# A hybrid decoder layer: weights and x loaded in half blocks in the order of use, adaLN summed by VectorE and TensorE, and the list schedule's durations corrected

## The chip, the cores and the metric

The kernel runs on one core of one Trainium2 chip. The metric is the device time of one execution in microseconds. TensorE, VectorE, ScalarE, GpSimd and SyncE appear in the rows as PE, DVE, ACT, POOL and SP; SP issues most of the DMAs, ScalarE's queue a few small ones.

## What is computed

One layer on x of 4096 tokens by 1024 features, float32. The condition c gives, through a 1024 x 3072 matrix (`ada_w`), a shift, a scale and a gate:

```python
shift, scale, gate = jnp.split(c_act @ ada_w + ada_b, 3, axis=-1)
h = _rmsnorm(x, g_pre) * (1.0 + scale[:, None]) + shift[:, None]
proj = h @ w_in
...
y = jnp.concatenate([attn, rwkv, gla], axis=-1) @ w_out
return x + gate[:, None] * _rmsnorm(y, g_post)
```

Between the two lies a mixer of three groups of heads that all read h: sliding-window attention (window 128), RWKV-7 (a delta rule, in chunks of 64 tokens) and gated linear attention (GLA).

## The kernel before

The tokens are worked in 16 chunks of 256. A first half of the kernel makes h for each chunk, the RWKV and GLA projections and both recurrences, and leaves h (`hscr`) and the mixed heads (`mscr`) in DRAM. A second half reads h again and does attention, the gates, the output projection and the final norm. Every float32 weight is split into two float16 halves, a high and a low (`kh`, `kl` and so on), and so is h (`hT`): a projection is three matmuls per block of 128 features. A split of a weight (`load_w`) squares and sums it on ScalarE, sums over the partitions with a matmul by ones (`wssp`), makes a power of two from that on VectorE (`pow2`, a chain of operations of one column: `wtot`, `p2e`, `p2f`, `wsc`), writes the high half with ScalarE and the low half with VectorE.

Before the first chunk stands a start. The weights' blocks of 256 columns (1 MB each) come through four big buffers (`stg`: two with the tag AT, two with the tag hT). Eight blocks of `ada_w` are summed by VectorE, one step per block of 128 rows (`acc`), and a matmul by ones finishes each (`adp`). From them come `sh` and `gs`, and a common power of two, `hscale`. Then follow the splits of `gv` and `gk1` (GLA values and gate), `L` (the two low-rank inputs of RWKV, made from `wlt`), `k`, `r`, `v` and `gqk`. `wlt` lies in the only buffer of x (`xt`). The gate's four blocks of `ada_w` (`stage_g`) are multiplied and folded by GpSimd (`aw`, `acc`), summed with a matmul (`gp`), copied by VectorE (`gr`) and stored (`gscr`).

A chunk's stages: `stage_a` loads x, takes its norm (`ssx`, `msx`, `rsx`: a short chain on VectorE), scales x in place, transposes it on TensorE (`tp`), applies `gs` and `sh` on ScalarE (`hf`) and splits it into `hT`. `stage_p` does the projections: `pv` (gv and gk1), `lp` (L), `zz` three times (k, r, v), `gqk`; `stage_d` the decays, the other stages the recurrences. `cs` are pieces of the second half's weights, split on the way (`stage_c`).

The order of the work is made twice. `emit` runs the stages as generators and picks, by a rough model of the engines (`Model`, `Lane`), which goes on next; that fixes the order in which instructions are written. Each is noted in `Order` (`note`) with a duration, what it needs and its buffers. `pin` then schedules all that were noted with these durations, engine by engine, always the first written among those that are ready, and fixes each engine's order by dependencies without a semaphore. It is called once after the first half and once at the end. So a number in `note` moves instructions, and does no work itself. All instructions are recorded through one helper, line 299 before and 319 after, and so all rows have that line.

Of the kernel before, what the change touches and what calls it, by code (L numbers as in the profile page):

```python
# [16 lines left out]
ALU = mybir.AluOpType  # L17
# [16 lines left out]
LIFT = {}  # L34
LANES = ((0.06, 1.04e-3, VL), (0.02, 1.0e-3, AL), (0.1, 2.3e-3, 0.0), (0.0, 1e-3 / 2.4, PL), (0.05, 0.0, 2.0))
# [3 lines left out]
HOP_FROM = {"PE": 0.037, "DVE": 0.034, "Activation": 0.034, "Pool": 0.06, "SP": 0.03}  # L39
# [15 lines left out]
class Step:  # L55


    __slots__ = ("ins", "eng", "occ", "lat", "table", "array", "bytes", "needs", "turn", "start", "end", "left", "then")


class Order:
# [3 lines left out]
    def __init__(self, tc):  # L65
        self.tc, self.held, self.masks = tc, {}, {}
        self.steps = []
        self.wrote, self.read, self.users, self.slots, self.known = {}, {}, {}, {}, set()
# [26 lines left out]
    def note(self, eng, name, outs, ins, func, r):  # L95

        st = Step()
        st.ins, st.eng, st.table, st.array, st.bytes, st.then = r.ins, str(eng.engine).split(".")[-1], None, None, 0, []
        e, o = st.eng, outs[0]
# [3 lines left out]
        if e == "PE":  # L103
# [7 lines left out]
            took = max(took, 0.056 if not f32 else 0.109 if mode[1] == 4 else 0.0)  # L111
# [4 lines left out]
        elif e == "SP":  # L116
# [3 lines left out]
            st.lat = next((t for k, t in ((8, 1.9), (64, 2.0), (128, 2.2), (256, 2.6), (512, 3.5)) if kb <= k), 4.8)  # L120
# [32 lines left out]
        out_r, in_r = [self.region(a) for a in outs], [self.region(a) for a in ins]  # L153
        tiles = {a.tensor.name: a.tensor for a in [*outs, *ins]}
# [53 lines left out]
    def pin(self):  # L208
# [10 lines left out]
        cells, mode, table, pipe = [0.0] * 16, None, None, 0.0  # L219
        last = {}  # L220
        for _ in steps:
            e = min((e for e in ENGINES if ready[e]), key=lambda e: max(free[e], min(ready[e].values())))
            now = max(free[e], min(ready[e].values())) + 1e-9
            k = min(k for k, t in ready[e].items() if t <= now)
# [10 lines left out]
            else:  # L235
                if st.table is not None and st.table != table:
                    t, table = max(t, free[e] + 1.28), st.table
                free[e], st.end = t + st.occ, t + st.lat
                if st.bytes > 100e3:
                    pipe = max(pipe, t + 1.7) + st.bytes / 310e3  # L240
                    st.end = max(st.end, pipe)
# [22 lines left out]
class Model:  # L264


    def __init__(self, tc):
        self.tc, self.lift, self.order = tc, 0, Order(tc)
        self.wrote, self.read, self.banks = {}, {}, {}
        self.now = 0.0  # L270
# [15 lines left out]
class Lane:  # L286
# [6 lines left out]
    def __getattr__(self, name):  # L293
        f = getattr(self.eng, name)

        def call(*args, **kw):
# [6 lines left out]
            accum = kw.get("accum_out")  # L303
            self.model.order.note(self.eng, name, aps[:1] + ([] if accum is None else [accum]),
# [31 lines left out]
            end = t + took + self.late  # L336
            for o in outs:
                m.wrote[o] = (end, self)
# [18 lines left out]
def hybrid_kernel(ctx, tc, x, vecs, rows, adaw, w1, wl, w2, wo, w2aug, a2, gk2, cst, ctr, ctg, abias, out):  # L357
# [149 lines left out]
    def emit():  # L507

        while live:
# [13 lines left out]
            model.lift = LIFT.get(best[2], 0)  # L523
# [18 lines left out]

    def ada_block(eng, acc, aw, cc):

        SP.dma_start(aw, adaw[cc])
        if eng is V:
            V.tensor_scalar(acc, aw[:, 0, :], scol[:, 0:1], None, op0=ALU.mult)
            for k in range(1, KD):
                V.scalar_tensor_tensor(acc, aw[:, k, :], scol[:, k : k + 1], acc, op0=ALU.mult, op1=ALU.add)
        else:  # L550
            eng.tensor_tensor(aw, aw, scol.rearrange("p (k o) -> p k o", o=1).to_broadcast([P, KD, 256]), op=ALU.mult)
            eng.tensor_tensor(aw[:, 0:4, :], aw[:, 0:4, :], aw[:, 4:8, :], op=ALU.add)
            eng.tensor_tensor(aw[:, 0:2, :], aw[:, 0:2, :], aw[:, 2:4, :], op=ALU.add)
            eng.tensor_tensor(acc, aw[:, 0, :], aw[:, 1, :], op=ALU.add)
# [52 lines left out]
    with ExitStack() as p1:  # L607
# [26 lines left out]

        stc = itertools.count()

        def stage_tile(width=256):
            if next(stc) % 4 < 2:
                t = t_A([P, 2048], "stg")
            else:  # L640
                t = t_hT("stg").rearrange("p a k n -> p (a k n)").bitcast(F32)
            return t.rearrange("p (k c) -> p k c", k=KD)
# [24 lines left out]


        adp = pst("at", "adp")
        for cc in (4, 5, 6, 7, 0, 1, 2, 3):  # L670
            acc = cs1([P, 256], "acc")
            ada_block(V, acc, stage_tile(), cc)
            for jj in range(2):
                j = 2 * cc + jj
                PE.matmul(adp[:, j : j + 1], acc[:, jj * P : (jj + 1) * P], ones[:, 0:1], start=True, stop=True)
        V.tensor_add(sh, adp[:, 0:8], vcol("bsh"))
# [13 lines left out]


        Wt = {}
        wlt = t_x("wlt")[:, 0, :].rearrange("p (k c) -> p k c", k=KD)
        SP.dma_start(wlt, wl)

        def gen_l(s32):
            for k in range(KD):
                V.tensor_scalar(s32[:, k, 128:192], wlt[:, k, 0:64], vcol("muw", k), None, op0=ALU.mult)
                V.tensor_scalar(s32[:, k, 192:256], wlt[:, k, 64:128], vcol("mua", k), None, op0=ALU.mult)
            V.tensor_sub(s32[:, :, 0:128], wlt, s32[:, :, 128:256])  # L700

        gvh = wk1[0].tile([P, KD, 272], F16, name="gvh")
        gvl = wk1[0].tile([P, KD, 272], F16, name="gvl")
        for n, name in ((0, "gv"), (5, "gk1"), (None, "L"), (2, "k"), (3, "r"), (4, "v"), (1, "gqk")):
            inv = cp.tile([P, 1], F32, name="iv" + name)
            if name == "gk1":
                Wt[name] = (gvh, gvl, inv)
                load_w(gvh[:, :, 256:272], gvl[:, :, 256:272], inv, wt([P, KD, 16], "gk1s", 1, tag="gl"), src=w1src(n))
            elif name == "gv":
                Wt[name] = (gvh, gvl, inv)  # L710
                load_w(gvh[:, :, 0:256], gvl[:, :, 0:256], inv, stage_tile(), src=w1src(n))
            else:
                Wt[name] = (wslot(name + "h"), wslot(name + "l"), inv)
                if name == "L":
                    load_w(*Wt[name], stage_tile(), gen=gen_l)
                else:
                    load_w(*Wt[name], stage_tile(), src=w1src(n))
            V.tensor_scalar(inv, inv, hinv, None, op0=ALU.mult)
        gq_s = cp.tile([P, 1], F32, name="gq_s")
        V.tensor_single_scalar(gq_s, Wt["gqk"][2], 32.0 ** -0.5, op=ALU.mult)  # L720
        mu_s = pp.tile([P, 6], F32, name="mu_s")
        mu_c = pp.tile([P, 6], F32, name="mu_c")
        V.tensor_scalar(mu_c, vcol("mu"), -1.0, 1.0, op0=ALU.mult, op1=ALU.add)
        for n, nm in enumerate("rkv"):
            js = slice(2 * n, 2 * n + 2)
            V.tensor_scalar(mu_s[:, js], vcol("mu")[:, js], Wt[nm][2], None, op0=ALU.mult)
            V.tensor_scalar(mu_c[:, js], mu_c[:, js], Wt[nm][2], None, op0=ALU.mult)
# [92 lines left out]
        def stage_g(_):  # L820

            for n in range(4):
                acc = cs1([P, 256], "acc")
                aw = t_A([P, KD, 256], "aw")
                ada_block(G, acc, aw, 8 + n)
                gp2 = mq("gp2")
                PE.matmul(gp2[:, :256], ones, acc, start=True, stop=True)
# [979 lines left out]
```

## Time and profile before

| | us |
|---|---|
| median of 3 runs | 2227.8 (2226.26 to 2230.65) |
| profiled execution, own time | 2226.16 |
| its span, first to last instruction | 2224.4 |
| TensorE busy | 2063.7 (93%) |
| VectorE busy | 1513.7 (68%) |
| ScalarE busy | 1111.6 (50%) |
| GpSimd busy | 191.6 (9%) |
| mean DMA rate | 85 GB/s |

A timeline row gives the start and the duration in microseconds, the engine, the line, the operation, what is written and read, the shapes and a count; in brackets stands how long the engine idled before it and what ended that. A count of float32 matmuls in the trace is twice that of the program, since each is recorded as two passes. A window's row gives for each engine its busy time and instructions, then the granted clock of TensorE (1.00 is full), the share of the DMA engines and their rate.

### The profile page before, as it was taken

Reading aid. Unit: us, or ns where it says so; the run is one execution under the profiler, and the core shown is the slowest. Engines: PE = TensorE matmul, PEld = TensorE weight load, DVE = VectorE, ACT = ScalarE, POOL = GpSimd, SP = SyncE. Lnnn points to the kernel's source line nnn. Section 1 sums busy time; section 2 is a strip of 40 time slices with the busy share of each in tenths; the row PEclk is TensorE's granted clock in tenths of the full one; section 3 lists DMA queues with packets and bytes.
Section 4 is the critical chain, followed back from the end, with each engine's and each line's share of the span. In section 5 each row is a group of like instructions: output and inputs, shape, how many; then the busy total and the mean of one; then the engine's idle time right before and its main releaser. Section 6 shows DMA issues by size and latency. Waiting matters only on the chain. (4 is left out here: it accounts for less than half of the span.)

```text
span 2224.4 us, 61651 instructions
## 1 busy us (share of the span) xinstructions
PE 2063.7 (93%) x25417; PEld 1755.6 (79%) x25417; DVE 1513.7 (68%) x4970; ACT 1111.6 (50%) x2627; POOL 191.6 (9%) x364
## 2 busy tenths in 40 slices
PE   1599999999999999999997999999999999999996
PEld 1478877777777777787776888888888888888885
DVE  7767787777778777666665676666666666666764
ACT  3566666676766765555423434343434434343441
POOL 0241100111111111111000000000000000000000
PEclk9899999999999999999998999999999999999998
DMA  7332233323233322102324121222221121212111
GB/s 292 118 100 94 80 97 100 97 88 111 77 103 102 97 90 71 54 16 76 124 76 137 63 89 51 70 70 76 71 78 62 56 68 67 78 69 80 61 42 38
DMA packets 149092, 188.46 MB, mean 85 GB/s; under 512 B 49458, under 2 KB 120648, under 8 KB 142408
## 3 DMA queue, kind: packets, MB, share of 16 engines
q1 hardware_dynamic: 146776, 182.23, 24.9%
q8 instruction: 201, 3.29, 0.6%
q10 hardware_dynamic: 2032, 2.26, 0.3%
q14 instruction: 83, 0.68, 0.1%
HBM read 126.75 MB, written 57.68 MB: 83 GB/s over the span
## 5 line engine op out<-in xcount | busy, mean ns | idle before, releaser
L299 PEld LDWEIGHTS <-mT 128*128 128x128 f16 x3072 | 301.3, 98 | 40.1 <-ACT mT L299 2.6
L299 ACT ACTIVATE pr<-pr,nm,lsc 128x256 f32<-128x256 f32 (+1 forms) x256 | 149.3, 585 | 88.7 <-DVE nm L299 86.7
L299 ACT ACTIVATE ag<-gp,gh 128x512 f32<-128x512 f32 x64 | 43.6, 682 | 185.5 <-PE gp L299 185.4
L299 PEld LDWEIGHTS <-hT 128*128 128x128 f16 x1536 | 119.5, 100 | 18.9 <-DVE hT L299 1.0
L299 DVE CUSTOM_DVE_ANT_0 pr<-sc,ab,sinks 128x256 f32<-128x256 f32 (+1 forms) x256 | 107.8, 477 | 37.6 <-PE sc L299 35.9
L299 DVE SCALAR_TENSOR_TENSOR ag<-ag,gp 128x512 f32<-128x512 f32 x64 | 43.5, 679 | 110.7 <-ACT ag L299 110.6
L299 PE MATMUL pv<-gvh,hT 128*128 128x272 f16 x512 | 100.4, 287 | 0.7 <-DVE hT L299 0.4
L299 PE MATMUL lp<-hT,Lh 128*128 128x256 f16 x512 | 96.1, 279 | 2.4 <-ACT vg L299 2.4
L299 PE MATMUL op<-o0h,mT 128*128 128x256 f16 x512 | 93.4, 276 | 3.6 <-ACT mT L299 2.5
L299 PE MATMUL zz<-hT,kh 128*128 128x256 f16 x512 | 92.3, 276 | 0.0
L299 PE MATMUL gp<-hT,q3h 128*128 128x256 f16 x512 | 88.0, 278 | 3.6 <-PEq L1669 3.6
L299 PE MATMUL op<-o3h,mT 128*128 128x256 f16 x512 | 91.4, 273 | 0.0
L299 ACT ACTIVATE jy<-yv 128x1024 f16<-128x1024 f32 x32 | 33.8, 1057 | 114.0 <-DVE yv L299 114.0
L299 PE MATMUL gqk<-hT,gqkh 128*128 128x256 f16 x512 | 88.1, 273 | 1.9 <-DVE zb L299 1.9
L299 PE MATMUL qp<-hT,q1h 128*128 128x256 f16 x512 | 85.5, 274 | 4.2 <-DVE kT L299 4.2
L299 PE MATMUL op<-o2h,mT 128*128 128x256 f16 x512 | 89.3, 273 | 0.0
L299 PE MATMUL op<-o1h,mT 128*128 128x256 f16 x512 | 89.1, 273 | 0.0
L299 POOL COPY kT<-kT 128x512 f16<-128x512 f16 x15 | 10.1, 676 | 909.6 <-DVE kT L299 853.1
L299 PE MATMUL zz<-hT,rh 128*128 128x256 f16 x512 | 86.7, 273 | 0.0
L299 PE MATMUL zz<-hT,vh 128*128 128x256 f16 x512 | 86.4, 273 | 0.0
L299 ACT ACT_TABLE_LOAD x65 | 83.4, 1283 | 5.4 <-DMA sinks<-in_rows 4.2
L299 PE MATMUL gp<-hT,q4h 128*128 128x256 f16 x512 | 85.7, 273 | 0.0
(385 smaller groups left out, 6318.8 us busy)
## 6 DMA issues: line engine op xcount, KB each, us to landing
xt<-in_x SPq DMA_DIRECT2D x16, 1024.0 KB, 5.0
hscr<-hT SPq DMA_DIRECT2D x16, 1024.0 KB, 7.0
hT<-hscr SPq DMA_DIRECT2D x16, 1024.0 KB, 4.8
xo<-in_x SPq DMA_DIRECT2D x16, 1024.0 KB, 5.5
out<-yv SPq DMA_DIRECT2D x32, 512.0 KB, 3.0
cs<-in_w SPq DMA_DIRECT2D x112, 128.0 KB, 2.2
stg<-in_adaw SPq DMA_DIRECT2D x8, 1024.0 KB, 7.6
cs<-in_wo SPq DMA_DIRECT2D x64, 128.0 KB, 2.2
```

What stands on the lines that cost most here:

```text
L299: r = f(*args, **kw)
```

## The change

Three things are changed together.

The start. Weights and adaLN blocks come in halves of 0.5 MB through eight buffers (`half_tile`: the buffers that chunk 0 uses later for RA, UV, KB and AT), in the order in which they are used: gv, gk1, `wlt`, x of chunk 0, then adaLN, then k, r, v, gqk. VectorE sums six blocks of adaLN; blocks 5 and 1 go to TensorE as matmuls of one column against `scol` (`adp<-scol,stg`). The splits of gv, gk1 and L (`early`) and the norm of x are written between the adaLN steps. The splits of k, r, v and gqk become a stream of their own (`stage_l`), and the gate's sums (`stage_g`) use eight halves in place of four blocks. Chunk 0's transposes use four PSUM banks.

```diff
+        RING = ("RA", "UV", "KB", "RA", "AT", "AT", "AT", "AT")
...
+        gvp = w_pieces(0)
+        gks = wt([P, KD, 16], "gk1s", 1, tag="gl")
+        SP.dma_start(gks, w1src(5))
+        wlt = half_tile().rearrange("p (k c) -> p k c", k=KD)
+        SP.dma_start(wlt, wl)
+        load_x(0)
...
-        for cc in (4, 5, 6, 7, 0, 1, 2, 3):
+        first = early()
+        for n, cc in enumerate((4, 5, 0, 6, 7, 1, 2, 3)):
+            if cc in PE_BLOCKS:
+                for jj in range(2):
+                    aw = half_tile().rearrange("p (k c) -> p k c", k=KD)
+                    SP.dma_start(aw, adaw[cc, :, :, jj * P : (jj + 1) * P])
+                    for k in range(KD):
+                        PE.matmul(adp[:, 2 * cc + jj : 2 * cc + jj + 1], aw[:, k, :], scol[:, k : k + 1], start=(k == 0),
+                                  stop=(k == KD - 1))
+                    next(first, None)
+                continue
             acc = cs1([P, 256], "acc")
-            ada_block(V, acc, stage_tile(), cc)
+            for h in range(2):
+                aw = half_tile().rearrange("p (k c) -> p k c", k=4)
+                SP.dma_start(aw, adaw[cc, :, 4 * h : 4 * h + 4, :])
...
-            for n in range(4):
-                acc = cs1([P, 256], "acc")
-                aw = t_A([P, KD, 256], "aw")
-                ada_block(G, acc, aw, 8 + n)
+            for n in range(8):
+                aw = half_tile("AT").rearrange("p (k c) -> p k c", k=KD)
+                SP.dma_start(aw, adaw[8 + n // 2, :, :, (n % 2) * P : (n % 2 + 1) * P])
+                acc = cs1([P, P], "acc")
...
+        streams((9, "l", stage_l, None))
```

The list schedule. A ready instruction is no longer taken by the place at which it was written alone, but by that place and a lag: those of `stage_l` count as 150 places later, those of `stage_g` as 500 (`LAG`). Where TensorE would have to change its tiling, it takes a ready instruction of the present tiling first (for up to 0.6 in the schedule's time, if that is the full array). Some durations are corrected, of which two lines show the kind, and VectorE and ScalarE get a small pause where the half of the partitions changes.

```diff
-HOP_FROM = {"PE": 0.037, "DVE": 0.034, "Activation": 0.034, "Pool": 0.06, "SP": 0.03}
+HOP_FROM = {"PE": 0.037, "DVE": 0.034, "Activation": 0.034, "Pool": 0.06, "SP": 0.6}
...
-            k = min(k for k, t in ready[e].items() if t <= now)
+            at = sorted((k for k, t in ready[e].items() if t <= now), key=lambda k: (steps[k].rank, k))
+            k = at[0]
+            if e == "PE" and mode is not None and steps[k].array[0] != mode:
```

The model of `emit`. Large loads share one DMA rate there in the first half (`m.pipe`).

How the instructions move is shown at three places. First SP's queue at the start, before (`in_adaw` is `ada_w`, `in_w` the weights):

```order
L299 DMA stg<-in_adaw 128x2048 x4
L299 DMA wlt<-in_wl 128x1024
L299 DMA gk1s<-in_w 128x128
L299 DMA cs<-in_w 128x256 x2
L299 DMA stg<-in_adaw 128x2048 x3
L299 DMA cs<-in_w 128x256 x2
L299 DMA stg<-in_adaw 128x2048
L299 DMA stg<-in_w 128x2048
L299 DMA cs<-in_w 128x256 x2
L299 DMA stg<-in_w 128x2048 x2
L299 DMA xt<-in_x 128x2x1024
```

and now, the first two being gv:

```order
L319 DMA stgRA<-in_w 128x1024
L319 DMA stgUV<-in_w 128x1024
L319 DMA gk1s<-in_w 128x128
L319 DMA stgKB<-in_wl 128x1024
L319 DMA xt<-in_x 128x2x1024
L319 DMA stgRA<-in_adaw 128x1024
L319 DMA stg<-in_adaw 128x1024
L319 DMA stg<-in_adaw 128x8x128 x2
```

gv, `wlt` and x have moved ahead of all of adaLN.

Second VectorE's queue where x of chunk 0 is scaled, before (it stands behind adaLN, between the splits of L and k):

```order
L299 SCALAR_TENSOR_TENSOR rsx<-nwt,rsx 128x2
L299 TENSOR_TENSOR nwt<-rsx 128x2
L299 SCALAR_TENSOR_TENSOR nwt<-nwt,msx 128x2
L299 SCALAR_TENSOR_TENSOR rsx<-nwt,rsx 128x2
L299 TENSOR_SCALAR xt<-xt,rsx 128x1024 x2
L299 SCALAR_TENSOR_TENSOR kl<-stg,wsc,kh 128x2048
```

and now:

```order
L319 TENSOR_SCALAR acc<-stgUV,scol 128x256
L319 TENSOR_SCALAR xt<-xt,rsx 128x1024
L319 SCALAR_TENSOR_TENSOR acc<-stgUV,scol,acc 128x256
L319 TENSOR_SCALAR xt<-xt,rsx 128x1024
L319 SCALAR_TENSOR_TENSOR acc<-stgUV,scol,acc 128x256 x2
L319 SCALAR_TENSOR_TENSOR acc<-stgKB,scol,acc 128x256 x3
```

The scaling has moved in among the adaLN steps, with half of them still to come.

Third TensorE's queue in chunk 0's projections, before, in the projection of k (`cgp` belongs to GLA's decay; the gate's sums `gp<-acc` stand one by one further back, in the projections of k, r and gqk):

```order
L299 MATMUL zz<-hT,kh 128x256
L299 MATMUL tp<-ident,xt 128x128 x4
L299 MATMUL cgp<-CTG,gl 128x129 x2
L299 LDWEIGHTS kh
L299 MATMUL zz<-hT,kh 128x256
```

and now, between the last matmul of k's projection and the first of r's (`tp` is of chunk 1):

```order
L319 MATMUL zz<-hT,kl 128x256
L319 MATMUL gp_476<-acc,ones 128x128
L319 MATMUL wssp<-wss_655,ones 128x2
L319 MATMUL gp_487<-acc,ones 128x128
L319 MATMUL tp<-ident,xt 128x128 x4
L319 MATMUL zp<-ident,vg 17x128 x2
L319 MATMUL gp<-gk2s,zlT 128x128 x2
L319 MATMUL gp_499<-acc,ones 128x128
L319 MATMUL tp<-ident,xt 128x128 x4
L319 MATMUL gp_510<-acc,ones 128x128
L319 LDWEIGHTS rh
L319 MATMUL zz<-hT,rh 128x256
```

Four of the gate's eight sums now stand together ahead of the whole projection of r, and chunk 1's transposes and decay stand among them.

More of the change, by code (lines that the diff above doesn't have):

```diff
@@ L702, in hybrid_kernel @@
[L702 to L718, printed above, removed]
```

190 lines of the change are left out of this document (136 added, 54 removed).

## The prediction

> **What bounds the kernel now.** I read the stages first (busy time by window), then what TensorE waits for, then the start instruction by instruction.
>
> ```profile
> span 2224.4 us, 61651 instructions
> core 0: us, PE busy (x) PEld busy (x) DVE busy (x) ACT busy (x) POOL busy (x), PEclk, DMA share, GB/s
> 20.00:25.00 5.00, 1.01 (x4) 0.93 (x4) 4.75 (x11) 0.91 (x4) 0.00 (x0) 1.00 1.04 423
> 0.00:62.40 62.40, 13.55 (x53) 11.87 (x54) 49.26 (x172) 23.39 (x43) 3.31 (x18) 1.00 0.75 280
> 79.00:97.00 18.00, 2.64 (x23) 2.13 (x23) 17.58 (x15) 2.05 (x6) 16.57 (x9) 0.76 0.43 157
> 97.00:136.20 39.20, 36.97 (x273) 30.70 (x274) 22.55 (x42) 21.59 (x43) 16.52 (x14) 0.89 0.21 81
> 136.20:1085.00 948.80, 908.32 (x12144) 741.14 (x12141) 696.47 (x2529) 598.83 (x1386) 136.69 (x292) 0.99 0.28 85
> 1254.00:2190.00 936.00, 924.15 (x10710) 825.08 (x10707) 604.84 (x1808) 385.39 (x971) 8.93 (x13) 1.00 0.20 67
> ```
>
> From 136 us on TensorE carries the time: it is busy 908 of 949 us in the first half and 924 of 936 in the second. Before that it is starved: 48.9 us idle up to the first projection at 62.4, and 15.4 of the 18 us from 79 to 97. So the start is worth what it delays TensorE's unbroken run, and I follow one mark, the first projection of chunk 1 (`pv`, 136.19). What is gained there is kept if the middle's idle 40.5 us do not grow. What TensorE waits for, first up to 130 us, then in the middle:
>
> ```profile
> PE adp L299 <- DVE acc L299: 33.8, 8, 13.1
> PE tp L299 <- DVE xt L299: 18.1, 3, 13.8
> PE cgp L299 <- DVE gl L299: 7.3, 6, 2.7
> ```
>
> VectorE makes the adaLN sums at the start; the scaled x of chunk 1 costs one wait of 13.8; the middle has many short ones. The start in rows:
>
> ```profile
> 10.65 0.39 ACTq L666 DMA_DIRECT2D bdm<-in_cst  x1
> 13.10 1.01 PE L299 MATMUL adp<-ones,acc 128*128 128x1 f32 x4 [13.10 <-DVE acc L299]
> 20.91 0.35 DVE L299 TENSOR_SCALAR acc<-stg,scol 128x256 f32<-128x256 f32 x1
> 32.14 0.35 DVE L299 TENSOR_SCALAR acc<-stg,scol 128x256 f32<-128x256 f32 x1
> 33.19 0.25 DVE L299 TENSOR_SCALAR stg<-wlt,vt 128x64 f32<-128x64 f32 x1
> 33.75 0.25 DVE L299 TENSOR_SCALAR stg<-wlt,vt 128x64 f32<-128x64 f32 x1
> 35.93 1.91 ACT L299 ACTIVATE gvh<-stg 128x2048 f16<-128x2048 f32 x1 [5.26 <-DMA stg<-in_w]
> 41.32 1.22 DVE L299 TENSOR_TENSOR stg<-wlt,stg 128x1024 f32<-128x1024 f32 x1
> 42.47 0.16 DVE L299 TENSOR_TENSOR sh<-adp,vt 128x8 f32<-128x8 f32 x1
> 42.57 0.38 SPq L299 DMA_DIRECT2D xt<-in_x  x1
> 46.04 0.23 DVE L299 TENSOR_SCALAR sh<-sh,hscale 128x8 f32<-128x8 f32 x1
> 48.89 2.35 DVE L299 SCALAR_TENSOR_TENSOR gvl<-stg,wsc,gvh 128x2048 f16<-128x2048 f32 x1
> 54.65 0.16 DVE L299 COPY wtot<-wssp 128x1 f32<-128x1 f32 x1 [0.88 <-PE wssp L299]
> 57.92 1.42 DVE L299 TENSOR_SCALAR xt<-xt,rsx 128x1024 f32<-128x1024 f32 x2
> 60.33 1.02 ACT L299 ACTIVATE hf<-tp,sh,gs 128x256 f32<-128x256 f32 x2 [0.46 <-PE tp L299]
> 74.02 0.33 SPq L299 DMA_DIRECT2D aw<-in_adaw  x1
> 74.96 0.63 ACT L299 ACTIVATE hT<-hf 128x512 f16<-128x512 f32 x1
> 75.78 0.68 DVE L299 TENSOR_TENSOR hT<-hf,hT 128x512 f16<-128x512 f32 x1
> 78.53 0.28 PE L299 MATMUL pv<-gvh,hT 128*128 128x272 f16 x1
> 79.21 4.41 POOL L299 TENSOR_TENSOR aw<-aw,scol 128x2048 f32<-128x2048 f32 x1 [65.62 <-DMA aw<-in_adaw]
> ```
>
> adaLN's shift and scale stand at 46.3, but x was sent for only at 42.57 (its buffer held `wlt`), so h begins (`hf`) 14 us later.
>
> **The adaLN sums.** VectorE keeps six of eight blocks, and now also does ahead of them the splits of gv, gk1, L and the norm of x that came after. First work: ScalarE's queue still issues its loads first (end 11.0), then two half squares (1.91 for the whole, read-out 0.2 each, 2.3) and TensorE's sum, 0.6: about 13.7. VectorE's list up to the last adaLN step: 48 steps at 0.47 (three blocks of 8 from 20.91 to 32.14), 22.5; 16 products for L, 0.1 each in the steps' shadow (step and product together 0.56, the spacing at 33.19), 1.6; their subtractions 1.2; splits of gv and L 2 x 2.35 and gk1, 5.1; scaling x 1.4; some 37 short ones, 0.15 each in a chain (22 from 54.65 to 57.92), half hidden between longer ones, 3. Sum 34.8; 32 if more hides, 37 if nothing does. Last step at 48.5, TensorE adds it by 49.5, and then the same 3.8 as before (42.47 to 46.27): `hf` at 53.4 against 60.33, **6.9 earlier**, 5 to 10.
>
> TensorE's two blocks are 32 products of one column, 0.5 each (two in 1.01): 8 us a block, on an engine idle 48.9 of 62.4. Without that cover, the second block, read last at about 48, would delay the mark by up to 2. Loads: some 12.5 MB before shift and scale (adaLN 8.4, gv, `wlt` and x 2.6, small ones 1.5), 30 us at the 423 GB/s of 20 to 25 us; VectorE's list ends later, so loads in halves cost nothing while several are in flight.
>
> **h and the first projection.** Before, `hf` to the last `hT` takes 16.1 us, because ScalarE does whole weights of 2 us in between. Now its queue holds 8 `hf` (0.51), 4 casts (0.63) and three half weights (1.0): 9.6, and the last difference 0.7. `hT` at 63.7, `pv` done 65.2 against 78.8: **13.6 earlier**.
>
> **From there to the middle.** Here the change adds a wait. In TensorE's queue the four first gate sums stand before the r projection, so GpSimd's results release it; in VectorE's queue the gate copies stand before chunk 1's short chain, in SP's the gate's halves before x of chunk 1.
>
> ```profile
> 87.35 3.60 POOL L299 TENSOR_TENSOR aw<-aw,scol 128x2048 f32<-128x2048 f32 x1
> 87.44 3.53 DVE L299 SCALAR_TENSOR_TENSOR rsx<-nwt,rsx 128x2 f32<-128x2 f32 x1
> 91.59 2.33 POOL L299 TENSOR_TENSOR aw<-aw 128x1024 f32<-128x1024 f32 x1
> 94.00 1.26 POOL L299 TENSOR_TENSOR aw<-aw 128x512 f32<-128x512 f32 x1
> 95.34 0.72 POOL L299 TENSOR_TENSOR acc<-aw 128x256 f32<-128x256 f32 x1
> 96.11 1.42 DVE L299 TENSOR_SCALAR xt<-xt,rsx 128x1024 f32<-128x1024 f32 x2
> 104.64 0.63 PE L299 MATMUL lp<-hT,Lh 128*128 128x256 f16 x2
> 112.72 0.38 PE L299 MATMUL zz<-hT,rh 128*128 128x256 f16 x2
> 136.19 0.28 PE L299 MATMUL pv<-gvh,hT 128*128 128x272 f16 x1
> ```
>
> GpSimd's long operations hold VectorE: a step of 128 x 2 lasts 3.53 beside a 3.60 one, and this last step but six of x's chain and the six behind it, 0.15 each elsewhere, take from 87.44 to 96.11. Then the new order by these rows: the low half of r is split at about 69, which frees the first gate pair's buffer; its loads go at 69.5, x of chunk 1 behind them at 70.2. A load of 1 MB alone took 5.2 (74.02 to 79.21), and 2.1 MB need 2.5 more: x at 76.5. ScalarE stands on that x, with the squares of v behind it, so v is split by 85; only then are gate halves three and four loaded, there by 89. GpSimd needs for them two products of 1.8, two sums each of 1.3 and 0.7, and last sums of 0.4: the fourth gate sum at 97, the r projection at 99 against 112.72, **13.7 earlier**.
>
> From there to chunk 1 took 23.5. Add 2: TensorE has idled about 10 us, and after such a wait it ran matmuls 0.21 apart, up to about 105 (5.7 us), instead of 0.11 (two in 0.63 at 104.64, in 0.38 at 112.72), 2.8 lost, part of which smaller gate sums and free VectorE time return. The mark falls at 124.5: **11.7 earlier**. Ends: 5, if the remaining gate halves (17 us of GpSimd) hold VectorE's `zb`, and 17, if the list needs 32 and the gates do not stop TensorE.
>
> The Trainium skill, "TensorE: Matmul & The Clock Gate", Part 1, puts the slow stretch after idling at about 3.4 us. By that the loss would be 1.7, and the lead an estimated 1 us longer; the trace's 5.7 us of slow matmuls differ, and decide.
>
> **The middle and the end.** The first half's instructions are re-sorted throughout, by corrected durations and by staying in TensorE's current tiling. No row prices that. Bounds: nothing below the 40.5 us of idle can go, and the named waits are short (`cgp` 7.3 in six); I take 0, within -8 and +8, because orders with equal work shift such waits more than they remove them. In the second half TensorE's sequence stays as it was: 0.
>
> Sum: 11.7 off the profiled execution's 2226.16 (1.8 of it outside the span). The median of the runs is 1.6 higher, 2227.8, and the forecast is made on it: **2216**, own range 2208 to 2224 by the ends of the lead and a part of the middle's.
>
> **The rivals.** (1) The middle gains as well: if the waits for `cgp` and half as much again of its likes go, 10 us more, **2206**. For it: the waits are misjudged chains; against it: they sit at 1 to 3 us, in a queue without slack. (2) The gates eat the lead: GpSimd and VectorE take turns, so VectorE's work between (x scaling 1.4, `zb`, some 15 short ones) adds itself to GpSimd's 17 us and the loads come 3 later; from the r projection starting after 108 the gain is under 4.5, **2224**. For it: rows 87.35 and 87.44; against: halves release VectorE every 1.8 instead of 3.6. (3) **Slower**: in the re-sorted middle, chain results come behind TensorE's next need. It decides at 16.2 us (11.7 and 4.5) over 15 chunks, 1.1 us more idle in each beside the present 2.7: **2234**. For it: the short waits of the middle turn on fractions of a microsecond; against: 95.7% busy leaves little to misplace. (4) Halves are slow to load: 5.2 less 2.5 leaves 2.7 a load that no byte pays. If that stood beside nothing, 19 half loads of 3.95 and x would hold `hf` to about 87, 27 later than before, of which the later steps return 5: **2250**. Against: 423 GB/s with two or three loads in flight. The Trainium skill, "DMA: Bandwidth & Descriptors", Bandwidth, asks for transfers of a megabyte and more for three quarters of the peak, and so speaks against the change; the trace's 423 GB/s is for whole megabytes, and no row shows halves.
>
> **How the numbers follow.** Forecast 0.54, rival 1 0.20, rival 2 0.13, rival 3 0.10, rival 4 0.03. A measurement of this kernel can tell about 0.2% (4.5 us) from no change. Faster: forecast, rival 1 and the better third of rival 2, 0.78; same: the rest of rival 2, 0.09; slower: rivals 3 and 4, 0.13. The range, 2200 to 2228, leaves out the far part of rival 1 and rivals 3 and 4, about 2 in 10.
>
> **What would show it.** `hf` begins between 50 and 56, x scaled before; `pv` done by 67; TensorE's longest wait after that is for GpSimd's `acc`, ending at 97 to 101; `pv` of chunk 1 at 119 to 131; idle from there to the end of the first half within 8 us of 40.5. Wrong: `hf` after 58, the r projection after 108, or an idle middle of over 50 or under 32.

## The result, and the profile after

The changed kernel takes 2202.6 us (median; 2199.59 to 2204.35) against 2227.39 for the kernel before on the same chip: a ratio of 0.9885, 95% interval 0.9868 to 0.9902, so 24.8 us less. The forecast was 2216. The direction was right and the time lies in the range, but the gain is more than twice the 11.8 that was forecast (2227.8 to 2216), and the experiments below put it elsewhere than the forecast did.

The stages first. This is busy time by window for the kernel before; the cuts are the first `pv` of chunk 1, the last `yt` of the first half, and the first `op` of the second:

```profile
0.00:136.20 136.20, 66.22 (x407) 53.08 (x408) 101.65 (x263) 62.52 (x110) 36.40 (x41) 0.92 0.51 190
136.20:1178.00 1041.80, 992.24 (x13466) 808.99 (x13464) 750.71 (x2726) 628.93 (x1453) 145.67 (x309) 0.99 0.28 85
1178.00:1251.70 73.70, 55.77 (x632) 46.99 (x631) 42.71 (x140) 29.54 (x84) 0.61 (x1) 0.86 0.37 128
1251.70:2224.40 972.70, 949.49 (x10920) 846.48 (x10917) 618.58 (x1844) 390.64 (x980) 8.93 (x13) 0.99 0.19 66
```

And the same four stages of the changed kernel (columns: window, length, then busy time and instructions of TensorE, its weight loads, VectorE, ScalarE and GpSimd, then TensorE's granted clock, DMA share, GB/s); its profiled execution took 2204.35 us, with a span of 2202.6:

```profile
0.00:126.30 126.30, 75.04 (x466) 64.39 (x467) 72.83 (x247) 63.91 (x128) 41.20 (x57) 0.91 0.61 205
126.30:1155.60 1029.30, 998.49 (x13470) 817.11 (x13468) 747.06 (x2736) 627.60 (x1454) 146.49 (x309) 0.98 0.28 86
1155.60:1230.10 74.50, 56.23 (x632) 46.98 (x630) 42.68 (x140) 29.56 (x84) 0.61 (x1) 0.84 0.37 127
1230.10:2202.60 972.50, 949.23 (x10920) 846.36 (x10917) 617.44 (x1844) 390.83 (x980) 7.97 (x13) 0.99 0.19 66
```

Read down the first column of lengths: 9.9 us from the start (136.2 to 126.3), 12.5 from the middle, 0.8 lost in the transition, 0.2 gained in the second half. The middle's 12.5 are two things of opposite sign. TensorE's idle time (length less busy) falls from 49.6 to 30.8, 18.8 less; its busy time rises by 6.3, with 4 matmuls more out of 13,470, so not by work. Many short waits, of which the prediction showed one kind (`cgp`), are what went. TensorE's waits from 130 us to the first `op`, the kernel before (total, times, longest):

```profile
PE rp L299 <- DVE Sst L299: 5.3, 3, 2.8
PE Xp L299 <- DVE T L299: 4.6, 6, 0.9
PE bp L299 <- ACT UV L299: 3.2, 7, 0.5
PE sp L299 <- ACT UV L299: 2.3, 8, 0.3
```

and the changed kernel:

```profile
PE Xp L319 <- DVE T L319: 1.1, 1, 1.1
PE cgp L319 <- DVE gl L319: 0.6, 2, 0.4
PE rp L319 <- DVE Sst L319: 0.3, 1, 0.3
PE sp L319 <- ACT UV L319: 0.2, 1, 0.2
```

`cgp` for `gl` fell from 7.3 to 0.6, `rp` for `Sst` from 5.3 to 0.3, `Xp` for `T` from 4.6 to 1.1, `sp` for `UV` from 2.3 to 0.2, and `bp` no longer waits for `UV`: 20.5 us in five kinds of wait. Waits of other kinds grew a little, so that the whole fell by 18.8.

The busy time rose mostly because TensorE's clock was halved for 24 us in the last chunk of the first half. Windows of the changed kernel there:

```profile
1063.80:1067.00 3.20, 2.48 (x74) 1.80 (x74) 2.33 (x5) 0.00 (x0) 0.00 (x0) 1.00 0.83 333
1067.00:1091.00 24.00, 23.04 (x215) 16.55 (x216) 8.88 (x19) 2.92 (x8) 5.04 (x9) 0.50 0.04 6
1091.00:1096.00 5.00, 5.00 (x74) 3.43 (x74) 2.10 (x7) 1.26 (x4) 0.13 (x1) 1.00 0.09 25
```

A granted clock of 0.50 over 23 us of busy TensorE is some 11.5 us of work lost. Summed over windows of 4 us as busy time by (1 less the granted clock), the middle loses 16.5 us to slow clock after the change and 6.7 before. So the middle gained 18.8 us of idle time and paid 6.3 of busy time. The slow clock accounts for that rise; its own sum, 9.8 more than before, is larger than the rise, so it is a rough measure.

### The profile page after: what moved, and what is told of

Same layout as the page of the kernel before. It is cut to its first block, busy times and chain, and to the rows that moved or that the text cites. A ratio compares the mean times of both kernels' runs of the same rounds, so it can differ in the third digit from the quotient of the medians.

```text
span 2202.6 us, 61822 instructions
## 1 busy us (share of the span) xinstructions
PE 2079.0 (94%) x25481; PEld 1774.8 (81%) x25481; DVE 1480.0 (67%) x4965; ACT 1111.9 (50%) x2645; POOL 196.3 (9%) x380
## 5 line engine op out<-in xcount | busy, mean ns | idle before, releaser
L319 PEld LDWEIGHTS <-hT 128*128 128x128 f16 x1536 | 116.9, 98 | 18.6 <-DVE q L319 1.0
L319 PE MATMUL lp<-hT,Lh 128*128 128x256 f16 x512 | 89.4, 273 | 1.0 <-ACT vg L319 0.9
L319 PE MATMUL qp<-hT,q0h 128*128 128x256 f16 x512 | 87.6, 276 | 0.0
```

The source lines that it names most:

```text
L319: r = f(*args, **kw)
```

## The experiments

The runs were on several chips; the kernel before had medians of 2227.4 to 2232.3 beside them, so ratios to it are compared. "Mark" is the first `pv` of chunk 1 in the profiled run, "idle" TensorE's idle time from there to the last `yt`, "slow clock" the busy time lost to the clock in that stretch, as above. These three come from one profiled execution each, the ratio from medians.

| kernel | ratio (95%) | mark, us | idle, us | slow clock, us |
|---|---|---|---|---|
| before | 1 | 136.2 | 49.6 | 6.7 |
| changed | 0.9885 (0.9868 to 0.9902) | 126.3 | 30.8 | 16.5 |
| changed, once more (e12) | 0.9872 (0.9836 to 0.9909) | 128.4 | 32.5 | 16.0 |
| new start, old list (e1) | 1.0035 (1.002 to 1.0049) | 129.8 | 53.4 | 16.1 |
| old start, new list (e2) | 0.9882 (0.9868 to 0.9897) | 136.6 | 37.2 | 6.0 |
| old start, pause only (e5) | 1.0018 (1.0006 to 1.0031) | 136.6 | 50.5 | 8.5 |
| old start, tiling only (e6) | 0.9956 (0.9938 to 0.9973) | 134.9 | 45.8 | 11.1 |
| old start, DMA numbers only (e7) | 0.9963 (0.9952 to 0.9975) | 134.0 | 40.0 | 7.7 |
| old start, tiling and DMA (e10) | 0.9901 (0.988 to 0.9923) | 134.9 | 35.0 | 2.8 |
| changed, x of chunk 1 first (e3) | 0.9864 (0.9846 to 0.9882) | 114.0 | 34.4 | 14.7 |
| the same, splits without lag (e4) | 0.9927 (0.9914 to 0.994) | 119.4 | 42.0 | 14.2 |
| changed, no adaLN on TensorE (e8) | 0.9856 (0.9833 to 0.988) | 130.3 | 32.3 | 1.4 |
| the same, x of chunk 1 first (e9) | 0.984 (0.9817 to 0.9862) | 116.7 | 31.6 | 0.0 |
| changed, dense filler (e11) | 0.9869 (0.9837 to 0.9901) | 126.4 | 33.0 | 12.8 |
| e8 with 28 instructions more (e13) | 0.984 (0.9817 to 0.9863) | 127.8 | 33.1 | 0.0 |
| changed with 28 instructions more (e14) | 0.9899 (0.9877 to 0.9922) | 123.1 | 35.5 | 20.8 |
| one adaLN block, x first (e15) | 0.9833 (0.9809 to 0.9857) | 116.9 | 37.4 | 3.0 |

**Start and list apart.** The first run keeps the new start (with its lags and the change to `emit`) and gives the list schedule its old numbers:

```diff
-HOP_FROM = {"PE": 0.037, "DVE": 0.034, "Activation": 0.034, "Pool": 0.06, "SP": 0.6}
+HOP_FROM = {"PE": 0.037, "DVE": 0.034, "Activation": 0.034, "Pool": 0.06, "SP": 0.03}
...
-                if st.bytes:
+                if st.bytes > 100e3:
...
-                        t = max(t, free[e] + 0.115)
+                        t = max(t, free[e] + 0.0)
...
-            if e == "PE" and mode is not None and steps[k].array[0] != mode:
+            if False and e == "PE" and mode is not None and steps[k].array[0] != mode:
```

with the old latency table and matmul durations too. The second is the mirror of it, the kernel before with the new numbers and without the lags.

> New start (half tiles, order of loads, adaLN on VectorE and TensorE, gates in eight halves), but the list schedule works with the numbers of before: SyncE hop 0.03, the DMA table and the 100 KB bound of before, the matmul durations of before, no pause between partition halves, no preference for the same tiling. The changed kernel takes 2202.6, the kernel before 2227.4, a gain of 24.8, of which the prediction gave 11.4 to the start and 0 to the order. Theory A, the start is worth the 11 or 12 us forecast and the corrected durations bring the other 12 or 13: 2214 to 2218, TensorE idle about 40 us between the first pv of chunk 1 and fp, as before. Theory B, the start alone brings all of it and the order follows by itself: 2201 to 2206, idle about 21 us there. Theory C, the two need each other (the new order of loads is only good under the new durations): above 2220.

> The kernel before with its old start, but its list schedule works with the new numbers (SyncE hop 0.6, DMA table, all transfers in one pipe, matmul durations, pause of 0.115 between partition halves) and prefers the same tiling. Theory A, the order brings 12 or 13 us by itself: 2213 to 2217, TensorE idle 20 to 27 us between the first pv of chunk 1 and fp instead of 40.5. Theory B, it is the start: 2225 to 2230, idle about 40. Theory C, both are needed: 2225 to 2230 here and above 2220 in the run with the old numbers.

Measured: 2239.06 us, ratio 1.0035, for the new start with the old list, slower than before; 2205.76, ratio 0.9882, for the old start with the new list, which is the whole gain of the change. No theory as written: A had the right sign for the list but half its size and a gain for the start; B and C are out, since the list does its work with no help from the start. The middle of the two, first the old list under the new start:

```profile
129.80:1190.40 1060.60, 1007.19 (x13464) 815.36 (x13463) 749.64 (x2730) 628.45 (x1453) 143.70 (x309) 0.98 0.27 84
```

then the new list under the old start:

```profile
136.60:1161.90 1025.30, 988.05 (x13461) 813.85 (x13461) 748.92 (x2728) 625.62 (x1453) 149.30 (x310) 0.99 0.28 87
```

With the old list the middle takes 1060.6 us, 18.8 more than before the change: the start's lead of 6.4 us is spent three times over, 15.0 as busy time (9.4 of it slow clock) and 3.8 as idle time. With the new list it takes 1025.3, 16.5 less, with the mark where it was before.

**Which numbers of the list.** Three parts alone, under the old start: the pause, the tiling preference (its lines as in the change, with 0.6 written out), the DMA numbers; then the last two together.

```diff
+                if st.half is not None:
+                    was, half[e] = half.get(e, st.half), st.half
+                    if was[0] != st.half[0] or None not in (was[1], st.half[1]) and was[1] != st.half[1]:
+                        t = max(t, free[e] + 0.115)
```

> The kernel before with its old start and old durations; its list schedule only adds the pause of 0.115 us between instructions of VectorE or ScalarE that work on different partition halves. All the new numbers together, under the old start, gave a ratio of 0.9882 (26 us). Theory P, the pause is what the list lacked (the waits of before in the middle are nearly all for VectorE and ScalarE: cgp for gl 7.3 us, rp for Sst 5.0, Xp for T 4.6, bp and sp for UV 5.5): 2205 to 2215. Theory Q, fewer tiling changes and better DMA times are: 2222 to 2232 here. Theory N, each change of the numbers re-sorts the list by chance and parts do not add up: anything from 2205 to 2240, with the time set by how many half-clock stretches of TensorE lie in the first half.

```diff
+                same = [q for q in at if steps[q].array[0] == mode]
+                wait = max(now - ready[e][q] for q in at if steps[q].array[0] != mode)
+                if same and (mode != (4, 4) or wait < 0.6):
+                    k = same[0]
```

> The kernel before with its old start and old durations; TensorE's list only prefers an instruction of the tiling it is in (unless others waited 0.6 us). Theory P, the pause is what matters: 2222 to 2232. Theory Q, fewer tiling changes, at some 0.1 us each, bring the order's gain: 2208 to 2218, with 20 or more changes fewer in the first half. Theory N, chance: no relation to the number of changes.

```diff
-HOP_FROM = {"PE": 0.037, "DVE": 0.034, "Activation": 0.034, "Pool": 0.06, "SP": 0.03}
+HOP_FROM = {"PE": 0.037, "DVE": 0.034, "Activation": 0.034, "Pool": 0.06, "SP": 0.6}
...
-                if st.bytes > 100e3:
+                if st.bytes:
```

> The kernel before with its old start; only the DMA numbers of the list are the new ones (hop from SyncE 0.6, latency table, every transfer in the shared pipe). No wait of over 0.9 us in the middle of the kernel before ends on a DMA. Theories P and Q: 2222 to 2230. Theory R, the later times of the small transfers (Xs, td, AS) move the solves of each chunk and so take away the waits of Xp and rp: 2212 to 2220. Theory N, chance: outside 2222 to 2230 in either direction, with half-clock stretches that go with it.

> The kernel before with its old start; the list prefers the same tiling and has the new DMA numbers, but no pause between partition halves and the old matmul durations. Alone the two gave 0.9956 and 0.9963, all numbers together 0.9882, the pause alone 1.0018. If parts add: 0.992, 2212 against 2230. If the pause and the matmul durations are what make the order good once the others are there: 2209 to 2214. If the two alone make it: 2203 to 2207. If chance rules (theory N): outside all of these.

The pause alone, 2233.84, made the kernel slower by 0.06 to 0.31%, so theory P falls, although nearly all waits of the middle end on VectorE or ScalarE. The tiling preference gave 2219.23 (0.44% faster) and the DMA numbers 2221.67 (0.37%); together they gave 2207.56, 0.99%, where the parts add to 0.81% and all the numbers give 1.18%. Within the intervals the two add, and carry most of it; what the pause and the matmul durations put on top is not told apart from nothing. Theory N, chance, is unlikely as the whole story, since the parts add and four of the five orders with new numbers have less idle time in the middle than before; five orders do not exclude it. The stretch with both, 35.0 us idle against 49.6:

```profile
134.90:1159.80 1024.90, 989.88 (x13472) 811.30 (x13471) 750.88 (x2727) 627.35 (x1456) 150.75 (x314) 1.00 0.28 87
```

How the preference works is only partly seen: counted over TensorE's rows from 100 us to the first `op`, tiling changes fell by some 20 of about 680 with the preference alone, which at the 0.094 us that the list schedule books for one would be 2 us of the 10. And no long wait of the middle ends on a DMA in the trace of before: so the DMA numbers must act by what they place elsewhere, which no run followed further.

**The waits of the start.** In the changed kernel x of chunk 1 stood behind two gate halves on SyncE, which went at 68.3, and TensorE waited 9.0 us for the squares of v behind that x, then 9.9 for a gate sum. The list gets one more rule, gate loads come after the load of x of chunk 1:

```diff
+        x1 = [k for k, st in enumerate(steps) if st.eng == "SP" and st.bytes == 1 << 20 and not st.half][1:2]
+        for st in steps:
+            if x1 and st.gate and st.eng == "SP" and st.bytes == 1 << 19:
+                st.turn.append(x1[0])
```

> The changed kernel with one thing moved: the load of x of chunk 1 is issued on SyncE ahead of the gate loads, which in the changed kernel waited for their tiles until 68.3 with it behind them. Theory 1, the 9.0 us that TensorE waits for the squares of v (behind the squares of x of chunk 1 on ScalarE) go, and the gates come some 3 us later: 9 less 3, so 2195 to 2199. Theory 2, the gates become the longer wait by as much as the first is shortened, or the order after it pays it back: 2201 to 2205.

and in the next run also

```diff
-LAG = {"l": 150, "g": 500}
+LAG = {"l": 0, "g": 500}
```

> As the run before, and the splits of the late weights (k, r, v, gqk) have no lag in rank any more, so v is squared on ScalarE ahead of x of chunk 1. Theory 1, v no longer waits for x at all: 2193 to 2198. Theory 2, the splits now stand ahead of the first chunk's h on ScalarE and VectorE (some 8 us of work) and delay pv of chunk 0: 2200 to 2206.

Measured 2199.85 (0.9864) and 2214.11 (0.9927). The first is a little better than the changed kernel, with intervals that overlap, and in any case by less than its 12.3 us earlier mark: the middle took 1036.2 us instead of 1029.3. The second follows its theory 2, and more: splits of k and r stand ahead of the first chunk's first `hT` and most of its `hf`, and its idle time in the middle is 42.0.

**adaLN on TensorE.**

```diff
-PE_BLOCKS = (5, 1)
+PE_BLOCKS = ()
```

> The changed kernel with all eight adaLN blocks of shift and scale summed by VectorE (none by TensorE), all else as changed. VectorE gets two more blocks of 16 steps (half blocks) at 0.41 to 0.48 us, 3.3 us each, so h comes 5 to 7 us later than at 53.5. If a lead at the start passes through to the end: 2202.6 and 5 to 7, 2208 to 2210. If the lead of the start is lost on the way (the new start under the new list gained 0 to 5 us although its first pv of chunk 1 is 10.3 us earlier than under the old start): 2199 to 2205, or by the stretch of half clock at 1067 to 1091, which a shifted start may or may not meet: 2192 if it is not met.

2198.62, ratio 0.9856. The mark comes 4.0 us later than in the changed kernel, and the end 4.0 us earlier. The middle shows why, first the whole of it, then the place where the changed kernel ran at half clock, with the same instructions in TensorE's list:

```profile
130.30:1150.70 1020.40, 988.13 (x13471) 809.44 (x13470) 746.30 (x2736) 627.66 (x1454) 146.13 (x309) 1.00 0.28 87
1077.50:1097.00 19.50, 19.39 (x290) 14.27 (x291) 12.14 (x34) 4.18 (x12) 5.17 (x10) 1.00 0.07 13
```

290 matmuls in 19.4 us at full clock, where the changed kernel took 23.0 us for 215. Still, the expectation gave 2192 for a kernel that does not meet the stretch: the sum of slow clock fell by 15.1, but busy time in the middle only by 10.4, and idle time rose by 1.5. Without the half clock, does an earlier start count? Both edits together:

> The two edits that beat the changed kernel together: all eight adaLN blocks of shift and scale on VectorE, and x of chunk 1 loaded ahead of the gate loads. The one alone had a ratio of 0.9856, the other 0.9864, the changed kernel 0.9885. If a lead at the start counts as long as TensorE keeps its clock: the first pv of chunk 1 some 12 us earlier than without the second edit (118 instead of 130) and the whole at 2186 to 2192. If the middle gives a lead back whatever the clock does (x first had its pv of chunk 1 12.3 us earlier than the changed kernel and gained 5): 2193 to 2199.

```profile
116.70:1138.30 1021.60, 990.04 (x13475) 811.69 (x13474) 752.48 (x2738) 629.82 (x1456) 153.60 (x317) 1.00 0.29 88
```

2193.41, ratio 0.984, just inside the second expectation, that the middle gives a lead back whatever the clock does. In the profiled runs the mark is 13.6 us earlier than without the second edit and the middle only 1.2 longer, as if the lead passed where the clock holds. But the profiled run of this kernel is the fastest of its four (2187.99) and that of the other the slowest (2200.34); the medians differ by 5 us, with intervals that overlap. That the lead passes is not shown.

**What halves the clock.** At the fall the trace of the changed kernel shows a stop within one solve of 64 matmul records:

```profile
1064.36 0.43 PE L319 MATMUL atp<-RA,KB 64*64 64x128 f32 x2 [0.83 <-DVE RA L319]
1066.16 0.67 PE L319 MATMUL Xq<-td,Xs 32*32 32x32 f32 x55
1067.96 0.37 PE L319 MATMUL Xq<-td,Xs 32*32 32x32 f32 x9 [1.13 <-issue]
```

After the wait of 0.83 for `RA` comes one of 1.13 for nothing that the profile shows, and the last 9 records already run at half clock. To see if thin work trips the clock, dense matmuls were put in front:

```diff
         kp = pjt("kp")
+        for _ in range(16 if i == 0 else 0):
+            PE.matmul(kp[:, :NT], Wq[2][0][:, 0, 0:P], hT[:, 0, 0, :], start=True, stop=True)
```

> The changed kernel with 16 more matmuls of full tiling (f16, 128x256, 0.11 us each, 1.8 us in all, their result overwritten) in front of the first kp projection of the second half, just ahead of where TensorE's clock falls to half at 1067 for 24 us. Up to there the order is that of the changed kernel; after it the dense matmuls lie among the small ones. Theory H, a few microseconds of thin work (waits of 0.8 and 1.1 us among 32x32 and 64x64 matmuls) trip the clock and the thin work after it keeps it low: no stretch at half clock, or one of under 8 us, and 8 to 10 us less: 2192 to 2196. Theory I, the half clock comes from somewhere else (its place in time, the loads of hT and of the weights then): the stretch stays and the kernel is 2 us longer, 2203 to 2206.

> The changed kernel itself, once more beside the others on the same chip: ratio 0.987 to 0.990, the stretch of half clock from 1067 to 1091 again.

2203.63 (0.9869) with the filler and 2202.63 (0.9872) without, so nothing; the filler ran from 1066.9 to 1068.9, the clock fell at 1072.5 instead of 1067, at the same record of the solve:

```profile
1066.94 1.92 PE L319 MATMUL kp<-hT,q2h 128*128 128x256 f16 x16
1073.01 0.36 PE L319 MATMUL Xq<-td,Xs 32*32 32x32 f32 x9 [0.85 <-issue]
```

and the window behind it is as slow, and as busy, as in the changed kernel:

```profile
1072.50:1092.00 19.50, 18.99 (x195) 14.19 (x196) 6.34 (x14) 0.52 (x2) 3.77 (x8) 0.50 0.03 5
```

Theory H falls as it was put: dense work just ahead does not keep the clock. By then one thing tied the stretch down: all kernels with two adaLN blocks on TensorE had it, whatever their list, none of the others. Two runs put 28 more instructions in front of the first `pv`, to tell the instruction's number from the start's timing, and one kept a single block (`PE_BLOCKS = (1,)`, with x of chunk 1 first):

```diff
+                for _ in range(14 if i == 0 and a == 0 else 0):
+                    PE.matmul(pv[:, 0:16], hT[:, 0, 0, 0:P], gvh[:, 0, 0:16], start=True, stop=True)
```

> As the run without TensorE's adaLN blocks (ratio 0.9856, no stretch of half clock in the middle), with 14 more tiny f16 matmuls and their 14 weight loads in front of the first pv, so that every later TensorE instruction has the number that it has in the changed kernel; they take under 1 us. In all kernels with TensorE's blocks the Xq solve of the last chunk of the first half stopped for 0.8 to 1.1 us at about the 54th or 55th of its 64 records and the clock fell to half for 16 to 24 us; in the two without these blocks, with the same instructions around it, it did not stop. Theory J, the stop belongs to the instruction's number in TensorE's program (the stream is interrupted there): the stop comes back at the 55th record, the half clock with it, and the kernel is 8 to 12 us slower, ratio 0.989 to 0.991. Theory K, it comes from the start's timing or from the summed blocks: no stop, no stretch, ratio 0.985 to 0.987.

> The changed kernel, with the same 14 tiny matmuls and 14 weight loads in front of the first pv. Theory J: the stop moves 28 instructions earlier in the work, to the thin atp or kp work ahead of Xq, Xq itself runs through; whether the clock falls then is open (if the stop there counts as well: as the changed kernel, 0.987 to 0.989; if not: 0.982 to 0.985). Theory K: stop at the 55th record and stretch as in the changed kernel, 0.987 to 0.989.

> One adaLN block of shift and scale on TensorE instead of two, and x of chunk 1 loaded ahead of the gate loads. None on TensorE gave 0.984 with its first pv of chunk 1 at 116.7, two gave 0.9864 with 114.0. If the half clock is what lies between those two: without a stretch 0.983 to 0.985, with one 0.986 to 0.988. Theory J: the number of the instruction at the stop is that of the changed kernel, so it falls some 14 records of TensorE's program away from the 55th record of Xq.

Without the blocks and 28 instructions later, the solve runs through and the clock stays (2198.08, 0.984):

```profile
1074.69 0.75 PE L319 MATMUL Xq<-td,Xs 32*32 32x32 f32 x64
```

With the blocks and 28 later, the stop moves to the 42nd record, 22 before the end (2211.36, 0.9899):

```profile
1075.71 0.38 PE L319 MATMUL Xq<-td,Xs 32*32 32x32 f32 x22 [0.90 <-issue]
```

and the stretch stays:

```profile
1075.50:1096.00 20.50, 20.29 (x217) 14.63 (x219) 8.34 (x19) 2.40 (x6) 5.04 (x9) 0.53 0.04 6
```

The first run cannot decide on theory J, because it did not give the later instructions the numbers that they have in the changed kernel. Two blocks on TensorE make 112 rows more in the trace than none (`adp` has 176 rows against 64), and the run put back 28. Up to the start of the solve, the changed kernel and this run:

```profile
0.00:1066.16 1066.16, 991.78 (x12818) 819.08 (x12818) 774.32 (x2807) 672.50 (x1536) 180.96 (x352) 0.99 0.33 103
0.00:1074.69 1074.69, 979.70 (x12776) 806.32 (x12776) 782.50 (x2823) 672.82 (x1536) 177.74 (x352) 0.99 0.33 103
```

That is 42 matmuls and 42 weight loads fewer, so the number at which the changed kernel stops falls behind the solve here. The second run bears theory J out as to the place. Up to the end of the stop, the changed kernel and the run with the blocks and 28 instructions more:

```profile
0.00:1067.96 1067.96, 992.45 (x12873) 819.64 (x12873) 775.01 (x2808) 672.50 (x1536) 180.96 (x352) 0.99 0.33 103
0.00:1075.71 1075.71, 997.54 (x12875) 822.24 (x12875) 776.83 (x2808) 673.01 (x1536) 178.97 (x352) 0.97 0.33 103
```

The stop comes behind the same number of instructions, within 2 matmuls, and so 13 matmuls and 13 loads earlier in the solve. Counted over all of TensorE's rows, its sequencer's too, 26,049 or 26,050 stand ahead of it in all seven profiles with two blocks. In the six profiles with the old start a stop of this kind stands behind 25,793 or 25,794 rows, 256 fewer. K, which had the stop stay at the 55th record, falls as it was put. J was wrong that the solve would run through, as 28 rows are fewer than the solve has. And the number alone does not make a stop: without blocks, or with one, TensorE does not idle at it.

One block and x first has neither stop nor stretch: 2195.57, ratio 0.9833 (0.9809 to 0.9857). It is not told apart from the two runs without blocks at 0.984, but it is from the old start with the new list (0.9882, 0.9868 to 0.9897): in this form the new start brings some 0.5% of its own.

## Where the prediction was right and where it failed

**The start: right in its steps.** The steps of the changed kernel that the prediction had worked out:

```profile
13.77 0.16 DVE L319 TENSOR_REDUCE wtot<-wssp 128x1 f32<-128x2 f32 x1 [6.89 <-PE wssp L319]
47.02 0.48 DVE L319 SCALAR_TENSOR_TENSOR acc<-stgRA,scol,acc 128x256 f32<-128x256 f32 x1
49.46 0.17 DVE L319 TENSOR_TENSOR sh<-adp,vt 128x8 f32<-128x8 f32 x1 [1.96 <-PE adp L319]
53.49 1.48 ACT L319 ACTIVATE hf<-tp,sh,gs 128x256 f32<-128x256 f32 x3 [1.87 <-DVE p2e L319]
62.46 0.69 DVE L319 TENSOR_TENSOR hT<-hf,hT 128x512 f16<-128x512 f32 x1 [1.10 <-ACT hT L319]
80.64 0.59 PE L319 MATMUL wssp<-wss,ones 128*128 128x2 f32 x2 [9.03 <-ACT vh L319]
97.17 0.79 PE L319 MATMUL gp<-acc,ones 128*128 128x128 f32 x2 [9.87 <-POOL acc L319]
102.76 0.63 PE L319 MATMUL zz<-hT,rh 128*128 128x256 f16 x2
```

VectorE's first work at 13.77 (forecast 13.7), the last adaLN step ends at 47.5 (48.5), `hf` at 53.49 (53.4), the last `hT` at 63.15 (63.7), the wait for GpSimd's `acc` ends at 97.17 (97). The r projection came at 102.76, not 99: between the gate sums the list also placed transposes of chunk 1 and the `gp` projection, and TensorE ran at half clock from the wait to 104.6. From there to the mark it was 23.5 us, as before; the 2 us that the forecast added for slow matmuls are not on top of that, since most of that stretch lies ahead of the r projection. (The forecast took 5.7 us for such a stretch; in the kernel before it had lasted from 97.0 to 105.4.) The mark fell at 126.3 (124.5): 9.9 earlier instead of 11.7, well inside 5 to 17. The two misses, 3.8 late and 2 less to go, partly cancel. The slow stretch of the kernel before, then the wait and what follows it in the changed one:

```profile
97.00:105.40 8.40, 8.40 (x38) 6.29 (x39) 1.86 (x4) 4.85 (x9) 0.00 (x0) 0.50 0.00 0
97.17:102.76 5.59, 5.09 (x20) 4.27 (x21) 2.66 (x12) 3.89 (x7) 2.78 (x6) 0.50 0.66 186
```

**Half loads: right.** The rival of slow halves is out, although they do move fewer bytes: one window of the changed kernel's start has the DMA engines full at 336 GB/s, where whole blocks had 423, but VectorE was busy 4.96 of the 5 us.

```profile
20.00:25.00 5.00, 1.15 (x6) 1.15 (x6) 4.96 (x20) 1.21 (x3) 0.00 (x0) 1.00 1.00 336
```

**The middle: the step that failed.** The prediction said of the re-sorted order: "I take 0, within -8 and +8, because orders with equal work shift such waits more than they remove them." The runs show the reverse: the list's numbers alone are worth 1.18%, some 26 us, under the old start. In the prediction's own measure, from the mark to where 1085 stood before (the matmul `fp`, now at 1043.8, with 43 matmuls fewer ahead of it), idle time fell from 40.5 us to 20.9, far under the 32 that it had named as its own refutation:

```profile
126.30:1043.80 917.50, 896.64 (x12101) 737.60 (x12098) 687.97 (x2530) 595.52 (x1384) 136.98 (x291) 1.00 0.28 86
```

The bound was as wrong as the value: it showed one kind of short wait, 7.3 us, and took its likes as too short to matter, though five kinds gave up 20.5 us together. Rival 1, the middle gains as well, was the right mechanism, with 10 us for what was 19 of idle time. Why just these numbers make a better order is known only in part, as said above.

**"What is gained there is kept": wrong too.** The prediction let the start's lead pass to the end as long as idle time did not grow. With the list's new numbers in both, the changed kernel has its mark 10.3 us ahead of the old start's (e2) and 6.4 us less idle time in the middle, yet 10.4 us more busy time there, with 10.5 more in the sum of slow clock. The prediction had no term for TensorE's clock in the middle. By the medians the new start adds nothing that can be measured under the new list (0.9885 against 0.9882, each within some 0.15%), and under the old list it makes the kernel slower (1.0035). So the time in the range is in part luck: the forecast's gain at the start did not reach the end, and a gain of the order that it had put at 0 stood in its place.

**The second half, taken as 0: right**, 972.5 us after 972.7.

## What to carry to other kernels

Where a planner sets the order, add up all short waits of the bound engine that end on another engine's result before calling a re-sort worth nothing: in the five kinds that shrank each was under 3 us here, and together they gave up 20.5 us. Test a change of two parts with each part alone: here one part had all of the measured gain, and the other looked good only at the mark that I followed, until fewer adaLN blocks stood on TensorE. And when a run is to hold an instruction's number fixed, count the rows of the trace: here 28 were put back for 112. And follow a lead to the end in busy time as well as idle time, with the granted clock beside it.

## What the runs showed of the hardware that I had not expected

TensorE's clock stayed at half for 16 to 24 us in the last chunk of the first half although TensorE was busy 23.04 of 24 us, in all seven profiles with two adaLN blocks on TensorE; none of the ten others has a slow stretch of over 8 us there. The Trainium skill, "TensorE: Matmul & The Clock Gate", Part 1, has the clock back after some 3.4 us of sustained work. This stretch took up to seven times that, and the measurement decides. Much of the work in it is 32x32 and 64x64 tiles, but some 2 us of full-tile float32 matmuls (`op`, from 1080.94) ran inside it in the changed kernel without ending it. Whether small tiles count less for the clock no run tested.

What starts the stretch stays open. A stop of 0.8 to 1.1 us inside a solve came with it each time, at most 3 us ahead of the fall, but the kernel before stops there for 2.60 us without losing its clock:

```profile
1096.74 0.25 PE L299 MATMUL Xq<-td,Xs 32*32 32x32 f32 x4 [2.60 <-issue]
```

Where the stop stands goes by the number of TensorE's rows ahead of it. Two summed blocks, a thousand microseconds earlier, put row 26,050 inside the solve; with one block or none it falls behind the solve. Later stops of this kind stand behind 27,329 or 27,330 rows in two profiles and behind 27,585 to 27,587 in others, again whole multiples of 256 away, within 2. What TensorE waits for there, why it stops at some of these numbers and not at others, and why the clock fell after these stops and not after that of the kernel before, no run tells; 16 dense matmuls 3.6 us ahead of the fall did not prevent it.
